# Output projection of a hybrid attention/GLA layer: five of seven products summed in shared PSUM banks, residual loads in slots of their own, the norm's root on ScalarE

## The chip, the cores and the metric

The program runs on one core of one Trainium2 chip. The metric is the device time of one execution in microseconds (us). Three runs of the kernel before gave 1463.15, 1465.78 and 1466.69 us; the median is 1465.78 us. One further execution was taken with the profiler; all rows below come from it.

## The reference, cut to what matters

The layer reads x (1024 tokens by 2048), projects it once, runs sliding-window attention and gated linear attention on the result, and ends with an output projection, a residual and a LayerNorm. Only the end is touched by this change:

```python
y = jnp.einsum('bse,ed->bsd', jnp.concatenate([y_a, y_g], axis=-1), w_out[l])   # 1024x2048 by 2048x2048
x = _layer_norm(DN_ALPHA * x + y, ln_g[l], ln_b[l])                             # per token, over 2048 columns

def _layer_norm(z, g, b):
    zf = z.astype(jnp.float32)
    mu = jnp.mean(zf, axis=-1, keepdims=True)
    var = jnp.mean(jnp.square(zf - mu), axis=-1, keepdims=True)
    return ((zf - mu) * lax.rsqrt(var + LN_EPS) * g + b).astype(z.dtype)
```

## The kernel before

**Numbers.** Everything is float32. An operand is split into a high part (a cast on ScalarE, L113) and a low part (a subtraction on VectorE, L114), and a product of two operands takes three matmuls: high by high (L740), high by the weight's low (L741), low by high (L742).

**Seven products.** The output projection starts at L690, after the projection, the attention and the GLA are done. It cuts tokens, inner width and columns into two halves each and replaces eight block products by seven, in the order 1, 6, 7, 4, 5, 3, 2. Each product works on one operand of y (512 tokens, 8 blocks k of the inner width; `y_part`, L709; sums of y blocks on GpSimd, L716) and one of the weights (`w_parts`, L719; four loads of 512 KB for each 512 columns). A product has two column halves, fp 0 and 1, and four token blocks t. Its loops are fp, k, t with three matmuls inside: 2 x 8 x 4 x 3 = 192 matmuls of 128x512. The very last half, product 2 with fp 1, runs token by token (t outside, k inside), so that a token block can be normed while the next is multiplied; three of its eight weights have slots of their own (`w2_p`, tiles vh and vl).

**Sums.** Each half of a product accumulates in four of eight PSUM banks (pool mm has 3, pool op has 5), and the next half uses the other four. `collect` (L774) adds each bank into the result tiles. `pre` has eight tiles of 128x2048, pre_11395 to pre_11398 for the first four token blocks and pre_11399 to pre_11402 for the last four. Columns 0 to 1023 of the first are called c11, the rest c12; of the second c21 and c22. x's columns 0 to 1023 are loaded into pre beforehand.

**Residual.** The second half of x's columns is added late (`residual`, L768): for the last four token blocks after product 5, for the first four after product 3. It loads 512 KB into a slot of `raw` (L771), adds it on VectorE (L772) and takes two statistics (L766). The pool `raw` has 4 slots, and all weight loads (L728 for products 1, 2, 3; L731 for the others) use the same four.

**Norm.** `norm` (L744) aggregates the statistics, gets the reciprocal root by a power on GpSimd (L454) with four small VectorE steps behind it (L455 to L458), and scales: 608 of the 2048 columns on ScalarE and GpSimd (L751, L752, L756, L757), 1440 on VectorE (L761, L762, in three pieces of 480 for the very last block). Stores follow each piece (L758, L763).

**What sets the order.** The engines run their instructions in the order of the program. A scheduler with its own timeline lays that order down, engine by engine; splits and loads have a high priority. All DMAs are issued by one engine (SP, its rows are SPq) in that order. An issue that waits for a free slot holds up all issues behind it.

Of the kernel before, what the change touches and what calls it, by code (L numbers as in the profile page):

```python
# [7 lines left out]
F32 = mybir.dt.float32  # L8
# [68 lines left out]
def build(ctx: ExitStack, tc, xT, xr, w_e, w_v, w_gk, w_up, b_gk, cos_d, sin_d, cst_d, sinks, wn_d, w_out, g_d, b_d, out):  # L77
# [615 lines left out]
    w2_p = ctx.enter_context(tc.tile_pool(name="w2", bufs=3, reuse_waits="tile"))  # L693
# [4 lines left out]
    mhalf2 = lp.tile([P, 1], F32, name="mhalf2")  # L698
    G.memset(mhalf2, -0.5)
    mh[0] = mhalf2  # L700
# [18 lines left out]
    def w_parts(i, fp, pools):  # L719

        out = []
        for q in range(4):
            r = raw_p.tile([P, 2, 512], F32, name="raw", tag="raw")
            with tc.high_priority(2000):
                if i in (1, 2, 3):
                    eg, w = {1: (fp, 0), 2: (fp, 2), 3: (2 + fp, 2)}[i]
                    src = w_out[eg, w + q // 2][:, (q % 2) * 1024:(q % 2) * 1024 + 1024]
                    SP.dma_start(r, src.rearrange("p (u c) -> p u c", u=2))  # L728
                else:
                    j = {5: 0, 7: 1, 4: 2, 6: 3}[i]  # L730
                    SP.dma_start(r.rearrange("p u (h c) -> p (u h) c", h=2), td[fp][:, 4 * q:4 * q + 4, j])  # L731
            for u in range(2):
                pool, tag = pools(2 * q + u)
                out.append(split(r[:, u], pool, tag))
        return out

    def product(acc, y, w, t, k):
        (yh, yl), (wh, wl) = y, w
        c = slice(t * P, t * P + P)
        PE.matmul(acc, yh[:, c], wh, start=(k == 0), stop=False)  # L740
        PE.matmul(acc, yh[:, c], wl, start=False, stop=False)  # L741
        PE.matmul(acc, yl[:, c], wh, start=False, stop=(k == 7))  # L742

    def norm(tb, tail):  # L744
        z, r0 = pre[tb], tb * P
        mv = lp.tile([P, 2], F32, name="mv", tag="mv", bufs=2)
        V.bn_aggr(mv, stats[tb])
        nmu = lp.tile([P, 1], F32, name="nmu", tag="nmu", bufs=2)
        V.tensor_scalar(nmu, mv[:, 0:1], -1.0, None, ALU.mult)
        p = slice(0, POOLED)  # L750
# [7 lines left out]
        SP.dma_start(out[r0:r0 + P, p], z[:, p])  # L758
        for a, m in cols:
            c = slice(a, a + m)  # L760
            V.scalar_tensor_tensor(z[:, c], z[:, c], mv[:, 0:1], gb[:, c], ALU.subtract, ALU.mult)  # L761
            V.scalar_tensor_tensor(z[:, c], z[:, c], rs, bb[:, c], ALU.mult, ALU.add)  # L762
            SP.dma_start(out[r0:r0 + P, c], z[:, c])  # L763
# [4 lines left out]
    def residual(tb):  # L768

        r = raw_p.tile([P, 1024], F32, name="raw", tag="raw")  # L770
        SP.dma_start(r, xr[tb * P:tb * P + P, 1024:])  # L771
        V.scalar_tensor_tensor(pre[tb][:, 1024:], r, ALPHA, pre[tb][:, 1024:], ALU.mult, ALU.add)  # L772
        for eg in (2, 3):
            stat(tb, eg)  # L774

    def collect(i, fp, t, acc):
        lo, hi = slice(fp * 512, fp * 512 + 512), slice(1024 + fp * 512, 1024 + fp * 512 + 512)
        c11, c12, c21, c22 = pre[t][:, lo], pre[t][:, hi], pre[NB + t][:, lo], pre[NB + t][:, hi]
        if i == 1:
            A.copy(c12, acc)  # L780
            V.scalar_tensor_tensor(c11, c11, ALPHA, acc, ALU.mult, ALU.add)
        elif i == 6:
            V.tensor_tensor(c12, c12, acc, ALU.add)
        elif i == 7:
            V.tensor_tensor(c22, c12, acc, ALU.add)
        elif i == 4:
            V.scalar_tensor_tensor(c21, c21, ALPHA, acc, ALU.mult, ALU.add)
            G.tensor_tensor(c21, c21, c22, ALU.add)
            stat(NB + t, fp)
        elif i == 5:  # L790
            V.tensor_tensor(c22, c22, acc, ALU.add)
            V.tensor_tensor(c12, c12, acc, ALU.add)
            if fp:
                residual(NB + t)
                norm(NB + t, False)
        elif i == 3:
            V.tensor_tensor(c12, c12, acc, ALU.add)
            if fp:
                residual(t)
        else:  # L800
            V.tensor_tensor(c11, c11, acc, ALU.add)
            stat(t, fp)
            if fp:
                norm(t, t == NB - 1)

    count = 0
    for n, i in enumerate((1, 6, 7, 4, 5, 3, 2)):
# [4 lines left out]
        if i == 7:  # L812
            SP.dma_start(gb, g_d)
            SP.dma_start(bb, b_d)
        ys = []
        for fp in range(2):
            accs = []
            for t in range(NB):
                pool, tag = (mm, "mm") if count % 8 < 3 else (op, "op")
                accs.append(pool.tile([P, 512], F32, name="acco", tag=tag))  # L820
                count += 1
            last = i == 2 and fp == 1
            ws = w_parts(i, fp, lambda k: (w2_p, "v") if last and k > 4 else (w_p, "w"))
            for k in range(8):
                if fp == 0:
                    ys.append(y_part(i, k))
                if not last:
                    for t in range(NB):
                        product(accs[t], ys[k], ws[k], t, k)
            for t in range(NB):  # L830
                if last:
                    for k in range(8):
                        product(accs[t], ys[k], ws[k], t, k)
                collect(i, fp, t, accs[t])
# [44 lines left out]
```

## Time and profile before

| what | value |
|---|---|
| runs of the kernel before | 1463.15, 1465.78, 1466.69 us |
| profiled execution, own time | 1466.27 us |
| its span, first to last instruction | 1464.4 us |
| PE busy in the span | 97% |
| VectorE, ScalarE, GpSimd busy | 61%, 41%, 25% |
| mean granted TensorE clock | 0.987 |

The span is what the engines show; 1466.27 - 1464.4 = 1.87 us of the execution lie outside of it. A clock of 1.00 means that TensorE was granted its full speed (the level of 2.4 GHz). Matmuls are pipelined: each takes 0.39 us from start to end, but one starts about every 0.23 us, so starts are what one counts by.

### The profile page before, as it was taken

To read this page: it belongs to the slowest core of one execution; us is meant where nothing else is said; L and a number is where in the kernel's file an instruction comes from. 1 tells how busy PE (TensorE), PEld (TensorE's weight loads), DVE (VectorE), ACT (ScalarE), POOL (GpSimd) and SP (SyncE) were. 2 spreads that over 40 slices of the span, in tenths; PEclk is the share of its full clock that TensorE was granted. 3 is DMA by queue.
4 is the path that set the end of the run, shared out by engine and by line. 5 is a ranking of instruction groups with operands and counts; after the bars stand their busy time and mean duration, and the time that the engine had idled before them with its cause. 6 is when DMAs were issued, how large, how long until landed. Compare 5 with 4: busy or idle time off the path is not lost.

```text
span 1464.4 us, 23613 instructions
## 1 busy us (share of the span) xinstructions
PE 1419.3 (97%) x8992; PEld 1183.5 (81%) x8992; DVE 886.2 (61%) x1522; ACT 605.9 (41%) x1278; POOL 370.4 (25%) x373
## 2 busy tenths in 40 slices
PE   8999999999999999999999999999999999997984
PEld 5888788888888977888889888888988888885763
DVE  5566556555655665566556555655565555567968
ACT  5544345434434554444335435443553434322321
POOL 0132211212221122232211221310023231465505
PEclk9999999999999999999999999999999999998987
DMA  8243344343434346443344343433235967666642
GB/s 311 94 150 113 126 131 145 120 132 127 148 109 137 117 158 214 138 138 123 122 145 137 123 132 119 148 108 115 94 113 179 360 204 222 192 217 210 215 130 115
DMA packets 101392, 224.47 MB, mean 153 GB/s; under 512 B 11040, under 2 KB 44192, under 8 KB 101024
## 3 DMA queue, kind: packets, MB, share of 16 engines
q1 hardware_dynamic: 101280, 222.98, 46.0%
q8 instruction: 70, 1.15, 0.3%
q14 instruction: 42, 0.34, 0.1%
HBM read 184.66 MB, written 33.55 MB: 149 GB/s over the span
## 4 chain that ended last, share of the span: by engine, by line
PE 92%; DVE 5%; DMA 1%; issue 1%; POOL 1%; ACT 0%; SPq 0%; DVEq 0%; ACTq 0%
PE acc L172 17%; PE acc L174 17%; PE acc L173 17%; PE acco L740 6%; PE acco L741 6%; PE acco L742 6%; PE accv L186 4%; PE accv L188 4%; PE accv L187 4%; PE po L291 2%; PE pa L360 1%; PE ps L260 1%; PE ps L259 1%; PE pt L281 1%; PE lracc L310 1%; DVE pre L762 1%
## 5 line engine op out<-in xcount | busy, mean ns | idle before, releaser
L114 DVE TENSOR_TENSOR wl<-raw,wh 128x512 fp32r<-128x512 f32 x445 | 344.4, 781 | 270.2 <-ACT wh L113 245.6
L113 ACT CAST wh<-raw 128x512 fp32r<-128x512 f32 x445 | 272.2, 620 | 444.5 <-PE acc L173 279.6
L172 PE MATMUL acc<-xh,wh 128*128 128x512 f32 x1088 | 429.4, 396 | 6.6 <-ACT wh L113 6.6
L174 PE MATMUL acc<-xh,wl 128*128 128x512 f32 x1088 | 426.6, 392 | 0.0
L173 PE MATMUL acc<-xl,wh 128*128 128x512 f32 x1088 | 426.5, 392 | 0.0
L172 PEld LDWEIGHTS acc<-xh,wh 128*128 128x128 f32 x1088 | 204.7, 188 | 53.8 <-ACT wh L113 7.6
L174 PEld LDWEIGHTS acc<-xh,wl 128*128 128x128 f32 x1088 | 204.6, 188 | 44.7 <-issue 1.4
L173 PEld LDWEIGHTS acc<-xl,wh 128*128 128x128 f32 x1088 | 204.8, 188 | 43.0 <-issue 2.2
L740 PE MATMUL acco<-wh,xh 128*128 128x512 f32 x436 | 168.0, 395 | 14.6 <-ACT wh L113 14.6
L741 PE MATMUL acco<-wl,xh 128*128 128x512 f32 x436 | 171.8, 394 | 3.9 <-DVE wl L114 3.9
L742 PE MATMUL acco<-wh,xl 128*128 128x512 f32 x436 | 171.0, 393 | 0.0
L186 PE MATMUL accv<-wh,xh 128*128 128x256 f32 x512 | 145.3, 284 | 0.0
L188 PE MATMUL accv<-wh,xl 128*128 128x256 f32 x512 | 145.0, 283 | 0.0
L187 PE MATMUL accv<-wl,xh 128*128 128x256 f32 x512 | 144.8, 283 | 0.0
L716 POOL TENSOR_TENSOR yr<-yr 128x512 f32<-128x512 f32 x56 | 79.6, 1424 | 150.1 <-DMA yr<-yd 145.3
L740 PEld LDWEIGHTS acco<-wh,xh 128*128 128x128 f32 x436 | 82.7, 190 | 32.7 <-ACT wh L113 15.5
L741 PEld LDWEIGHTS acco<-wl,xh 128*128 128x128 f32 x436 | 82.9, 190 | 22.0 <-DVE wl L114 4.6
L186 PEld LDWEIGHTS accv<-wh,xh 128*128 128x128 f32 x512 | 98.1, 192 | 1.2 <-issue 0.7
L188 PEld LDWEIGHTS accv<-wh,xl 128*128 128x128 f32 x512 | 98.1, 192 | 0.6 <-issue 0.3
L187 PEld LDWEIGHTS accv<-wl,xh 128*128 128x128 f32 x512 | 98.2, 192 | 0.5
L742 PEld LDWEIGHTS acco<-wh,xl 128*128 128x128 f32 x436 | 83.0, 190 | 17.3
L278 POOL TENSOR_TENSOR s<-s,sm 128x512 f32<-128x512 f32 x32 | 37.2, 1163 | 214.0 <-DVE sm L277 111.5
(173 smaller groups left out, 1707.2 us busy)
## 6 DMA issues: line engine op xcount, KB each, us to landing
raw<-in_w_e_dram SPq DMA_DIRECT2D x134, 512.0 KB, 3.9
yr<-yd SPq DMA_DIRECT2D x112, 256.0 KB, 4.8
raw<-in_w_v_dram SPq DMA_DIRECT2D x32, 512.0 KB, 4.4
raw<-in_w_out_dram SPq DMA_DIRECT2D x128, 128.0 KB, 2.6
td<-raw SPq DMA_DIRECT2D x32, 512.0 KB, 3.5
raw<-td SPq DMA_DIRECT2D x32, 512.0 KB, 4.3
raw<-in_w_out_dram SPq DMA_DIRECT2D x24, 512.0 KB, 4.5
raw<-in_xT_dram SPq DMA_DIRECT2D x15, 512.0 KB, 4.7
```

Of the source, the lines that this page charges most:

```text
L113: A.copy(hi, src)
L114: V.tensor_tensor(lo, src, hi.bitcast(F32), ALU.subtract)
L172: PE.matmul(acc, wh[:, c], xh, start=(k == 0), stop=False)
L173: PE.matmul(acc, wh[:, c], xl, start=False, stop=False)
L174: PE.matmul(acc, wl[:, c], xh, start=False, stop=(k == KT - 1))
L186: PE.matmul(o, xh[:, t], wh[:, c], start=(k == 0 and tb % 2 == 0), stop=False, skip_group_check=True)
L187: PE.matmul(o, xh[:, t], wl[:, c], start=False, stop=False, skip_group_check=True)
L188: PE.matmul(o, xl[:, t], wh[:, c], start=False, stop=(k == KT - 1), skip_group_check=True)
L716: G.tensor_tensor(a, a, b, ALU.add if sign > 0 else ALU.subtract)
L740: PE.matmul(acc, yh[:, c], wh, start=(k == 0), stop=False)
L741: PE.matmul(acc, yh[:, c], wl, start=False, stop=False)
L742: PE.matmul(acc, yl[:, c], wh, start=False, stop=(k == 7))
```

## The change

- Products 1, 6, 7, 4 accumulate in the same eight banks without a restart, then products 5 and 3 do; product 2 is alone. In between the running sum is copied out or added where it is complete: after product 1 into c11, after 6 to c12 (a ScalarE copy), after 7 to c22 (a ScalarE copy), after 4 into c21; after 5 into c22, after 3 into c12, after 2 into c11. The VectorE adds of products 6 (L783), 7 (L785) and one of product 5 (L792), the GpSimd add of product 4 (L788) and the ScalarE copy of product 1 (L780) are gone; the two new ScalarE copies are there.
- The residual is loaded into two slots of its own (pool `res`) and is added at products 7 and 4, no longer after 5 and 3. Statistics of the columns 1024 and up are taken as soon as products 5 and 3 are added.
- The root is ScalarE's Sqrt, followed by a reciprocal and three small steps on VectorE. ScalarE scales and shifts its 608 columns in one instruction instead of two; both GpSimd steps follow behind it.
- The last four token blocks are stored as whole tiles of 1 MB, issued behind the loads of product 2's first half. The first four are stored as before.
- The three extra weight slots of the last half are gone.

```diff
+    r_p = ctx.enter_context(tc.tile_pool(name="res", bufs=2, reuse_waits="tile"))
-    w2_p = ctx.enter_context(tc.tile_pool(name="w2", bufs=3, reuse_waits="tile"))
...
-    def product(acc, y, w, t, k):
+    def product(acc, y, w, t, k, first, last):
...
+        PE.matmul(acc, yh[:, c], wh, start=(first and k == 0), stop=False, skip_group_check=True)
+        PE.matmul(acc, yh[:, c], wl, start=False, stop=False, skip_group_check=True)
+        PE.matmul(acc, yl[:, c], wh, start=False, stop=(last and k == 7), skip_group_check=True)
...
-        nmu = lp.tile([P, 1], F32, name="nmu", tag="nmu", bufs=2)
-        V.tensor_scalar(nmu, mv[:, 0:1], -1.0, None, ALU.mult)
-        A.activation(z[:, p], z[:, p], AF.Identity, bias=nmu)
-        G.tensor_tensor(z[:, p], z[:, p], gb[:, p], ALU.mult)
-        rs = rsqrt(lp, mv[:, 1:2], 1.0, LN_EPS, 1)
-        A.activation(z[:, p], z[:, p], AF.Copy, scale=rs)
-        G.tensor_tensor(z[:, p], z[:, p], bb[:, p], ALU.add)
...
+        with tc.high_priority():
+            A.activation(q, mv[:, 1:2], AF.Sqrt, bias=eps)
+        V.tensor_scalar(v, mv[:, 1:2], -0.5, -0.5 * LN_EPS, ALU.mult, ALU.add)
+        V.scalar_tensor_tensor(z[:, c], z[:, c], mv[:, 0:1], gb[:, c], ALU.subtract, ALU.mult)
+        V.reciprocal(rs, q)
+        V.scalar_tensor_tensor(q, rs, v, rs, ALU.mult, ALU.mult)
+        V.scalar_tensor_tensor(rs, q, 1.5, rs, ALU.add, ALU.mult)
+        V.scalar_tensor_tensor(nmr, mv[:, 0:1], -1.0, rs, ALU.mult, ALU.mult)
+        A.activation(z[:, p], z[:, p], AF.Identity, bias=nmr, scale=rs)
...
+        G.tensor_tensor(z[:, p], z[:, p], gb[:, p], ALU.mult)
+        G.tensor_tensor(z[:, p], z[:, p], bb[:, p], ALU.add)
+        if tb < NB:
+            SP.dma_start(out[r0:r0 + P, p], z[:, p])
+        else:
+            late.append(lambda: tc.keep_in_program_order(SP.dma_start(out[r0:r0 + P, :], z)))
...
-        r = raw_p.tile([P, 1024], F32, name="raw", tag="raw")
+        r = r_p.tile([P, 1024], F32, name="res", tag="res")
...
+    FIRST, LAST = (1, 5, 2), (4, 3, 2)
...
         if i == 1:
-            A.copy(c12, acc)
             V.scalar_tensor_tensor(c11, c11, ALPHA, acc, ALU.mult, ALU.add)
         elif i == 6:
-            V.tensor_tensor(c12, c12, acc, ALU.add)
+            A.copy(c12, acc)
         elif i == 7:
-            V.tensor_tensor(c22, c12, acc, ALU.add)
+            A.copy(c22, acc)
         elif i == 4:
             V.scalar_tensor_tensor(c21, c21, ALPHA, acc, ALU.mult, ALU.add)
-            G.tensor_tensor(c21, c21, c22, ALU.add)
             stat(NB + t, fp)
         elif i == 5:
             V.tensor_tensor(c22, c22, acc, ALU.add)
-            V.tensor_tensor(c12, c12, acc, ALU.add)
+            stat(NB + t, 2 + fp)
             if fp:
-                residual(NB + t)
                 norm(NB + t, False)
         elif i == 3:
             V.tensor_tensor(c12, c12, acc, ALU.add)
-            if fp:
-                residual(t)
+            stat(t, 2 + fp)
...
+        if i in (7, 4):
+            for t in range(NB):
+                residual(t + (NB if i == 4 else 0))
...
+            if i == 2 and fp == 0:
+                for f in late:
+                    f()
```

The scheduler lays the order anew. On SP, before, from the last y loads of the projection on to the first store of the first four token blocks (raw<-in_xr_dram is a residual, raw<-in_w_out_dram at the end are the eight weight loads of product 2, two for one pair of k):

```order
L771 DMA raw<-in_xr_dram 128x1024
L706 DMA yr<-yd_3_115 128x512
L771 DMA raw<-in_xr_dram 128x1024 x2
L758 DMA out_dram<-pre_11399 128x608
L763 DMA out_dram<-pre_11399 128x1440
L706 DMA yr<-yd_3_115 128x512
L758 DMA out_dram<-pre_11400 128x608
L763 DMA out_dram<-pre_11400 128x1440
L771 DMA raw<-in_xr_dram 128x1024
L763 DMA out_dram<-pre_11401 128x1440
L758 DMA out_dram<-pre_11401 128x608
L763 DMA out_dram<-pre_11402 128x1440
```

In the changed kernel the same stretch of SP reads (L727 is the weight load, L705 the y load, L773 the store of a whole tile):

```order
L705 DMA yr<-yd_3_115 128x512
L727 DMA raw<-in_w_out_dram 128x1024
L705 DMA yr<-yd_3_115 128x512 x2
L727 DMA raw<-in_w_out_dram 128x1024
L705 DMA yr<-yd_3_115 128x512
L773 DMA out_dram<-pre_11399 128x2048
L773 DMA out_dram<-pre_11400 128x2048
L727 DMA raw<-in_w_out_dram 128x1024 x2
L773 DMA out_dram<-pre_11401 128x2048
L727 DMA raw<-in_w_out_dram 128x1024
L773 DMA out_dram<-pre_11402 128x2048
L727 DMA raw<-in_w_out_dram 128x1024
```

Before, all eight weight loads of product 2 stood behind the residual loads and the last store of pre_11402. Now the four of its first half stand ahead of the four stores (two of them are shown), and the four of its second half among and behind them.

The residual loads now stand in SP's row around product 7 (td are the stored weight sums that products 7 and 4 read; res is the new pool):

```order
L705 DMA yr<-yd_0_112 128x512
L705 DMA yr<-yd_0_116 128x512
L783 DMA res<-in_xr_dram 128x1024 x2
L705 DMA yr<-yd_1_113 128x512
L730 DMA raw<-td_111 128x4x256
L705 DMA yr<-yd_1_117 128x512
L783 DMA res<-in_xr_dram 128x1024 x2
L730 DMA raw<-td_110 128x4x256
L705 DMA yr<-yd_1_113 128x512
L705 DMA yr<-yd_1_117 128x512
```

The first two residual loads stand further up and find both slots empty; these two pairs and one more pair at product 4 wait until VectorE has added the residual whose slot they take.

On VectorE at the very end, between the third and the fourth token block, before (L801 adds the product, L766 and L747 are statistics, L761 and L762 the two scaling steps):

```order
L761 SCALAR_TENSOR_TENSOR pre_11397<-pre_11397,mv,gb 128x1440
L455 TENSOR_TENSOR rt<-rr 128x1
L801 TENSOR_TENSOR pre_11398<-pre_11398,acco 128x512
L456 TENSOR_TENSOR rt<-rt,rv 128x1
L766 BN_STATS stats_11406<-pre_11398 128x6
L457 TENSOR_SCALAR rt<-rt 128x1
L747 BN_AGGR mv<-stats_11406 128x2
L458 TENSOR_TENSOR rr<-rr,rt 128x1
L749 TENSOR_SCALAR nmu<-mv 128x1
L762 SCALAR_TENSOR_TENSOR pre_11397<-pre_11397,rr,bb 128x1440
L453 TENSOR_SCALAR rv<-mv 128x1
L761 SCALAR_TENSOR_TENSOR pre_11398<-pre_11398,mv,gb 128x480 x3
```

In the changed kernel (L810 adds the product, L778 and L745 are statistics, L754 and L765 the scaling steps, L756 to L759 what follows the root):

```order
L754 SCALAR_TENSOR_TENSOR pre_11397<-pre_11397,mv,gb 128x1440
L756 RECIPROCAL rr<-rt 128x1
L810 TENSOR_TENSOR pre_11398<-pre_11398,acco 128x512
L757 SCALAR_TENSOR_TENSOR rt<-rr,rv 128x1
L778 BN_STATS stats_11406<-pre_11398 128x6
L758 SCALAR_TENSOR_TENSOR rr<-rt,rr 128x1
L745 BN_AGGR mv<-stats_11406 128x2
L759 SCALAR_TENSOR_TENSOR nmr<-mv,rr 128x1
L765 SCALAR_TENSOR_TENSOR pre_11397<-pre_11397,rr,bb 128x1440
L752 TENSOR_SCALAR rv<-mv 128x1
L754 SCALAR_TENSOR_TENSOR pre_11398<-pre_11398,mv,gb 128x1440
```

The large steps stand as before. What changed is which small step stands between them, and that the fourth block's first scaling step is one of 1440 columns.

## Rows read from the trace of the kernel before

**Rows 1.** The chain that ended last, by engine, from the page.

```profile
PE 92%; DVE 5%; DMA 1%; issue 1%; POOL 1%; ACT 0%; SPq 0%; DVEq 0%; ACTq 0%
```

**Rows 2.** Windows from product 7 to the end; the columns stand in the first line.

```profile
core 0: us, PE busy (x) PEld busy (x) DVE busy (x) ACT busy (x) POOL busy (x), PEclk, DMA share, GB/s
1160.00:1332.50 172.50, 172.50 (x763) 142.82 (x761) 101.14 (x139) 54.25 (x95) 71.06 (x51) 1.00 0.68 217
...
1338.90:1349.40 10.50, 6.50 (x17) 4.69 (x18) 10.50 (x14) 4.79 (x10) 5.99 (x3) 0.56 0.82 266
1349.40:1389.20 39.80, 39.80 (x177) 32.79 (x175) 39.80 (x63) 14.77 (x24) 20.72 (x12) 1.00 0.63 213
1389.20:1403.10 13.90, 5.39 (x14) 4.10 (x14) 13.90 (x21) 3.42 (x6) 1.34 (x1) 0.63 0.89 273
```

**Rows 3.** PE's waits from 1120 us on: total us, times, longest.

```profile
PE acco L740 <- ACT wh L113: 14.6, 2, 8.5
PE acco L741 <- DVE wl L114: 3.9, 1, 3.9
```

**Rows 4.** Timeline of PE: start, duration, instruction.

```profile
1323.64 0.39 PE L742 MATMUL acco<-wh,xl 128*128 128x512 f32 x1
...
1332.48 0.39 PE L742 MATMUL acco<-wh,xl 128*128 128x512 f32 x1
...
1434.76 0.39 PE L741 MATMUL acco<-wl,xh 128*128 128x512 f32 x1
...
1444.00 0.40 PE L742 MATMUL acco<-vh,xl 128*128 128x512 f32 x1
```

**Rows 5.** SP's waits, 1300 to 1405 us.

```profile
SPq L728 <- DVE pre L772: 23.7, 8, 11.3
```

**Rows 6.** Groups of VectorE from 1060 us on: count, busy us, mean ns, idle before.

```profile
L772 DVE SCALAR_TENSOR_TENSOR pre<-raw,pre 128x1024 f32<-128x1024 f32 x8 | 10.8, 1354 | 0.0
...
L792 DVE TENSOR_TENSOR pre<-pre,acco 128x512 f32<-128x512 f32 x8 | 5.4, 679 | 0.0
```

**Rows 7.** The same groups of ScalarE: the copy out of PSUM.

```profile
L780 ACT COPY pre<-acco 128x512 f32<-128x512 f32 x8 | 4.3, 593 | 0.0
```

**Rows 8.** DMA issues: count, KB each, median us to landing.

```profile
yr<-yd SPq DMA_DIRECT2D x112, 256.0 KB, 4.8
...
raw<-in_xr_dram SPq DMA_DIRECT2D x8, 512.0 KB, 4.0
```

**Rows 9.** Timeline of GpSimd in product 7: the sum of two y blocks.

```profile
1215.82 1.51 POOL L716 TENSOR_TENSOR yr<-yr 128x512 f32<-128x512 f32 x1 [2.21 <-DMA yr<-yd]
```

**Rows 10.** ScalarE over the whole span: a table load.

```profile
L332 ACT ACT_TABLE_LOAD x8 | 10.3, 1283 | 0.2
```

**Rows 11.** Timeline of the end, VectorE, GpSimd and SP.

```profile
1447.01 1.46 POOL L752 TENSOR_TENSOR pre<-pre,gb 128x608 f32<-128x608 f32 x1
1447.07 1.41 DVE L455 TENSOR_TENSOR rt<-rr 128x1 f32<-128x1 f32 x1 [0.44 <-POOL rr L454]
1448.41 0.67 DVE L801 TENSOR_TENSOR pre<-pre,acco 128x512 f32<-128x512 f32 x1
...
1450.29 1.71 DVE L762 SCALAR_TENSOR_TENSOR pre<-pre,rr,bb 128x1440 f32<-128x1440 f32 x1
...
1451.10 2.21 POOL L757 TENSOR_TENSOR pre<-pre,bb 128x608 f32<-128x608 f32 x1 [2.63 <-ACT pre L756]
...
1451.97 4.32 DVE L761 SCALAR_TENSOR_TENSOR pre<-pre,mv,gb 128x480 f32<-128x480 f32 x3
...
1453.28 1.88 POOL L752 TENSOR_TENSOR pre<-pre,gb 128x608 f32<-128x608 f32 x1
...
1455.12 0.96 POOL L454 TENSOR_TENSOR rr<-rv,mhalf 128x1 f32<-128x1 f32 x1
1456.22 0.14 DVE L455 TENSOR_TENSOR rt<-rr 128x1 f32<-128x1 f32 x1
...
1460.68 0.38 SPq L758 DMA_DIRECT2D out_dram<-pre  x1
```

More of the change, by code (lines that the diff above doesn't have):

```diff
@@ L697, in build @@
     bb = lp.tile([P, D], F32, name="bb")
-    mhalf2 = lp.tile([P, 1], F32, name="mhalf2")
-    G.memset(mhalf2, -0.5)
-    mh[0] = mhalf2
+    eps = lp.tile([P, 1], F32, name="eps")
+    G.memset(eps, LN_EPS)
     def y_raw(h, g, k, tag):
@@ L732, in w_parts @@
             for u in range(2):
-                pool, tag = pools(2 * q + u)
-                out.append(split(r[:, u], pool, tag))
+                out.append(split(r[:, u], w_p, "w"))
         return out
-    def product(acc, y, w, t, k):
+    def product(acc, y, w, t, k, first, last):
         (yh, yl), (wh, wl) = y, w
         c = slice(t * P, t * P + P)
-        PE.matmul(acc, yh[:, c], wh, start=(k == 0), stop=False)
-        PE.matmul(acc, yh[:, c], wl, start=False, stop=False)
-        PE.matmul(acc, yl[:, c], wh, start=False, stop=(k == 7))
+        PE.matmul(acc, yh[:, c], wh, start=(first and k == 0), stop=False, skip_group_check=True)
+        PE.matmul(acc, yh[:, c], wl, start=False, stop=False, skip_group_check=True)
+        PE.matmul(acc, yl[:, c], wh, start=False, stop=(last and k == 7), skip_group_check=True)
     def norm(tb, tail):
@@ L804, in collect @@
                 norm(t, t == NB - 1)
+    accs = {}
     count = 0
-    for n, i in enumerate((1, 6, 7, 4, 5, 3, 2)):
+    for i in (1, 6, 7, 4, 5, 3, 2):
         if i in (1, 4):
@@ L814, in build @@
             SP.dma_start(bb, b_d)
+        if i in (7, 4):
+            for t in range(NB):
+                residual(t + (NB if i == 4 else 0))
         ys = []
         for fp in range(2):
[L817 to L823, printed above, removed]
+            if i in FIRST:
+                for t in range(NB):
+                    pool, tag = (mm, "mm") if count % 8 < 3 else (op, "op")
+                    accs[fp, t] = pool.tile([P, 512], F32, name="acco", tag=tag)
+                    count += 1
+            ws = w_parts(i, fp)
+            by_token = i == 2 and fp == 1
             for k in range(8):
@@ L826, in build @@
                     ys.append(y_part(i, k))
-                if not last:
+                if not by_token:
                     for t in range(NB):
-                        product(accs[t], ys[k], ws[k], t, k)
+                        product(accs[fp, t], ys[k], ws[k], t, k, i in FIRST, i in LAST)
+            if i == 2 and fp == 0:
+                for f in late:
+                    f()
             for t in range(NB):
-                if last:
+                if by_token:
                     for k in range(8):
-                        product(accs[t], ys[k], ws[k], t, k)
-                collect(i, fp, t, accs[t])
+                        product(accs[fp, t], ys[k], ws[k], t, k, True, True)
+                collect(i, fp, t, accs[fp, t])
 def layouts(x, w_in, w_gk_up, b_gk, attn_sinks, gla_norm_w, w_out, ln_g, ln_b):
```

16 lines of the change are left out of this document (9 added, 7 removed).

## The prediction, made before the changed kernel had run

> **What bounds the kernel now.** I read the chain that ended last first: TensorE holds 92% of it, VectorE 5% [rows 1]. So an edit counts only where it lets TensorE go on sooner, or shortens what follows its last matmul. Next come TensorE's waits in the output projection. There are three in all: 14.6 us in two waits for the high part of a weight (8.5 and 6.1), and 3.9 us in one for a low part [rows 3], together 18.5 us. The windows tell where. From 1160 to 1332.5, which holds nearly all of products 6, 7, 4 and 5, TensorE is busy without a gap at clock 1.00. The gaps lie at the two borders behind it: where product 3 starts (ends 1349.4) and where product 2 starts (ends 1403.1). In both windows VectorE has no idle time, and the granted clock is 0.56 and 0.63, so that TensorE runs part of them at its lower level, 1.2 GHz [rows 2].
>
> The waits of the queue SP say why the weights are late. At L728, the weight load, it waits 23.7 us in eight waits for L772, the residual's add on VectorE [rows 5]. The residual takes slots of the pool that the weights load into, is added only when VectorE gets to it, and until then the next weight load can't start.
>
> What the stalls cost in all can be counted. Between the starts at 1323.64 and 1332.48 lie 39 steps of TensorE [rows 4]: 0.2267 us each. In the by-token half, 40 steps from 1434.76 to 1444.00 give 0.231. Products 3 and 2 are 2 x 192 = 384 matmuls, 96 of them by token. Undisturbed they last 288 x 0.2267 + 96 x 0.231 = 65.3 + 22.2 = 87.5 us. They begin at 1332.48 + 0.23 = 1332.71 and the last ends at 1444.40, which is 111.7 us. So 24.2 us are lost: 18.5 as waits, and 5.7 by the lower clock behind them, 2.85 for each border.
>
> **The change, part by part.**
>
> *Residual out of the weights' slots.* At the border to product 3 VectorE loses, by mean durations, four adds of product 5's second half (L792, 4 x 0.679 = 2.7 us, gone) and four residual adds (L772, 4 x 1.354 = 5.4 us, now done beside product 4) [rows 6]; at the border to product 2 the other four residual adds, 5.4 us. The weight loads then depend only on the split that frees the slot, as they do in products 6 to 5, where TensorE never waits [rows 2, 3]. SP's order agrees: the weight loads stand among the y loads, and the first half of product 2 stands ahead of every store. I take both stalls as gone with their clock loss: **-24.2 us**. The bounds: nothing gained if the stalls came from the full VectorE alone (it is full in both windows), and no more than 24.2, since TensorE has no other gap here.
>
> *What is late next.* With the stalls gone TensorE does product 3 in 43.5 us (192 x 0.2267). I replayed the changed order by hand with the durations of the trace. VectorE has about 44 us of work beside product 3 (splits, four norms, adds, statistics), but splits go first by priority and the norms can slip: their stores stand behind the loads of product 2's first half, the norms end some 17 to 41 us after product 5, and the second half's weight loads behind the stores go out at 31 to 45 and are needed at 46 to 62. That is a slack of 10 us and more, so I cost the 1 MB stores at nothing. If that cover goes, the wait falls on the last half.
>
> *Residual loads at products 7 and 4.* Six of the eight are issued as three pairs that wait for VectorE's add of an earlier residual, and y loads for products 7 and 4 stand behind them. An add is 1.35 us [rows 6], the load 4.0 to land, a y load 4.8 [rows 8], the sum of two y blocks on GpSimd 1.5 [rows 9]. In the replay the operands k = 4 to 7 of product 7 are ready 2.6 to 3.7 us before TensorE needs them, because TensorE takes some of the second column half ahead of them. Product 6 has 1 to 2 us of slack at its last k. Cost nothing; bounds 0 and a wait at each of two places (rival C).
>
> *Shared banks.* Products 6 and 7 are copied out by ScalarE, 0.593 us a bank [rows 7], 2.4 for the four of a half, before the next product may add into them. Half a product is 96 x 0.2267 = 21.8 us, and ScalarE is under half busy in that stretch [rows 2]: nothing. The VectorE and GpSimd adds that go lie beside a TensorE that is never idle there: nothing gained.
>
> *The root on ScalarE.* The order has one more table load, ahead of the first Sqrt at the start of product 3, and none later. Table loads last 1.283 us with 0.2 us idle ahead of eight of them [rows 10]. ScalarE is idle for more than half of the windows around [rows 2], so I take nothing; the bounds are 0 and 1.5 us.
>
> The Trainium skill speaks against this step: "ScalarE: Activation LUTs", section "What ACT_TABLE_LOAD costs", counts a drain of about 1.4 us on top of the load for every switch to a function of another set, and exp and sqrt lie in different sets. By that the one switch would be an estimated 2.7 us of ScalarE instead of 1.5; nothing in the rows above shows the drain, and with one switch the sum stays the same.
>
> *The tail.* Before, the span ends 20.0 us after the last matmul (1444.40 to 1464.4); the fourth block's add of the product starts 4.0 us after it, the last store is issued at 16.3 [rows 11]. What fills the tail is VectorE and GpSimd holding each other off. A step of one column on VectorE (L455) took 1.41 us next to a GpSimd step of 608 columns, and 0.14 without one; three pieces of 480 took 4.32 while two GpSimd steps of 2.21 and 1.88 ran [rows 11]. One behind the other they fit: GpSimd ends at 1453.31, 1.3 us after VectorE's step of 1440 columns ended at 1452.00, and VectorE's pieces fill the rest. So I replay with 1.65 us for a VectorE step of 1440 columns, 1.3 for a GpSimd step of 608, one at a time, and 0.65 for an add or a statistic that overlaps with either. A token block then costs 2 x 1.65 + 2 x 1.3 = 5.9 us of such steps plus about 1.1 that nothing covers: 7.0. The power on GpSimd (0.96 alone [rows 11]) is gone, but reciprocal and three steps wait in the same way. Also, the first token block ends later: the low part of the last weight now comes late, and TensorE puts off that k, so block 0 ends at matmul 35 of 96, not 24. In the replay the fourth block's add starts 3.4 us after the last matmul, its statistics end at 5.8, its large step at 10.5, its last GpSimd step at 16 to 16.6. Before, the last store was issued at 16.3. **Tail: 0**, with bounds of -6 and +1.5 us; I take 0 because the rows with the overlap are of this very stretch.
>
> The Trainium skill has the rule behind it: "SBUF — State Buffer", section "Who interferes with whom", says that VectorE and GpSimd share a port pair which one holds for a whole instruction when a VectorE operation with two SBUF inputs meets GpSimd. The 1.41 us row agrees with it; without the rule the tail would be that of rival B.
>
> **Sum.** 1464.4 - 24.2 + 0 = 1440.2 us of span, plus 1.87 outside of it = 1442.1 for an execution like the profiled one. That one took 1466.27, 0.49 above the median of 1465.78; so the median of the changed kernel is about **1441.5 us**.
>
> **The rivals.**
>
> *B, the tail gets shorter too.* If VectorE and GpSimd don't hold each other as in the replay, the four blocks follow the multiplication (a block per 24 x 0.231 = 5.5 us). Then the last block has left about 0.5 to its add, 6 us of VectorE steps and 3.5 of ScalarE and GpSimd: about 10 instead of 16. For it: the power is gone, and both GpSimd steps come at the end. Against it: the 4.32 us row. 1441.5 - 6 = 1435.5.
>
> *C, a new wait in front of TensorE.* One residual pair that costs SP a whole landing and an add more than replayed is 4.0 + 1.35 = 5.4 us, against a slack of 2.6: a wait of 2.8, and 2.85 for the lower clock behind it as at the old borders. One such place gives 1447, both products 1453. For it: small slack, and an order that doesn't know the true durations. Against it: no wait there before [rows 2], when y loads were as many.
>
> *D, slower.* Each of the three pairs holds SP until VectorE has added, VectorE has splits of higher priority ahead of that add, and behind the pair stand the y loads of the product that runs. If each costs TensorE as much as the longest of the old waits, 8.5 us [rows 3], with 2.85 for the clock, it is 3 x 11.35 = 34 us against 24 saved: 1475.5. It decides only if all three do so (two give 1464, no change). Against it: VectorE is idle for 71 of the 172.5 us of that stretch [rows 2], so an add is not long in coming.
>
> *E, the stalls stay.* VectorE is full in both windows. If its queue and not the slots decides, its norms and statistics still stand there and TensorE waits on: about 1464. Against it: the 23.7 us that SP waits for the residual's add [rows 5], and 8.1 us less work at the first border.
>
> **How the numbers follow.** Forecast 0.60 (by itself 1438 to 1445), B 0.15, C 0.16, E 0.04, D 0.05. The range of 1434 to 1452 holds the first three but for a tenth. What a measurement of this kernel can tell from no change is about 0.3%, 4.4 us: the forecast, B and C are faster; E, with the part of D in which two pairs stall, is the same; the rest of D is slower. Faster 0.91, same 0.04, slower 0.05.
>
> **What would show it.** Right: no wait of TensorE of over 1 us between product 5 and the end, clock 1.00 throughout, the last matmul about 24 us earlier; no wait of SP at the weight load for a residual's add; the tail still near 20 us with VectorE steps of over 2 us beside GpSimd. Wrong: a wait of TensorE for a split of y in products 7 or 4 (C, D), a wait for a weight at products 3 or 2 with VectorE full (E), a tail under 17 us (B).

## The result, and the profile after

The changed kernel took 1455.97 us (median of 4 runs, 1455.35 to 1460.07) against 1464.65 for the kernel before on the same chip: a ratio of 0.9946 with a 95% interval of 0.9923 to 0.9969, some 8.7 us faster. The forecast was 1441.5 with a range of 1434 to 1452, so the direction was right, and only 8.7 of the 24 us forecast came. A second set of five runs gave 1457.13 (0.9937, 0.9925 to 0.9950). The profiled execution took 1460.07 us, its span is 1458.1; it is the longest of the first four runs, which matters below.

The chain that ended last, from the page, beside [rows 1]:

```profile
PE 90%; DVE 4%; DMA 3%; POOL 1%; issue 1%; ACT 1%; SPq 0%; POOLq 0%; DVEq 0%; ACTq 0%
```

Loads have come into the chain where there was 1% before. The waits of TensorE from 1120 us on (total, times, longest), beside [rows 3]:

```profile
PE acco L740 <- DVE xl L114: 7.9, 2, 4.9
PE acco L738 <- ACT xh L113: 4.4, 1, 4.4
```

Not one wait for a weight is left: all 18.5 us of [rows 3] are gone. In their place stand three waits, 12.3 us, for the other operand: the high and low parts of y. The windows of product 7, product 3, product 2 and the tail, in the columns of [rows 2], show where:

```profile
1202.60:1252.10 49.50, 45.09 (x193) 36.86 (x192) 23.51 (x32) 20.16 (x37) 7.42 (x6) 0.97 0.72 216
1339.30:1395.30 56.00, 48.11 (x194) 38.64 (x193) 50.86 (x76) 22.08 (x39) 24.38 (x15) 0.91 0.58 195
1395.30:1439.20 43.90, 43.90 (x194) 36.03 (x192) 35.58 (x55) 8.68 (x16) 10.61 (x6) 1.00 0.30 108
1439.20:1458.10 18.90, 0.00 (x0) 0.00 (x0) 14.12 (x18) 1.98 (x3) 11.79 (x6) 0.59 0.42 166
```

A product undisturbed takes 43.5 us. Product 7 took 6.1 more (4.4 of wait, the rest at a lower clock), product 3 took 12.4 more (7.9 of wait, the rest clock), product 2 none. The tail is 18.9. Against the forecast span of 1440.2 this adds up: 6.6 us later at the start of product 3 (6.1 from product 7 and 0.5 from before it), 12.4 in product 3, 1.1 less in the tail: 1458.1.

**Product 7.** Timelines of SP, GpSimd and ScalarE (start, duration, instruction; L783 is the residual load):

```profile
1207.72 1.47 SPq L783 DMA_DIRECT2D res<-in_xr_dram  x2
1209.28 0.38 SPq L705 DMA_DIRECT2D yr<-yd  x1
1209.76 0.38 SPq L730 DMA_DIRECT2D raw<-td  x1
1210.23 0.46 SPq L705 DMA_DIRECT2D yr<-yd  x1
...
1219.28 1.26 POOL L715 TENSOR_TENSOR yr<-yr 128x512 f32<-128x512 f32 x1 [12.67 <-DMA yr<-yd]
...
1220.58 0.62 ACT L113 CAST xh<-yr 128x512 fp32r<-128x512 f32 x1 [8.73 <-POOL yr L715]
```

The y load issued at 1210.23 lands at 1219.1, after 8.9 us, where the median of [rows 8] was 4.8. Ahead of it, within 2.5 us, went two residuals of 512 KB, a weight sum of 512 KB and another y load. TensorE waits for that block until 1221.25. The load was also issued late: it stands on SP behind the residual pair, and the pair waited 7.1 us for VectorE's add of an earlier residual, which frees the slot. SP's waits for that add from 1195 to 1225 us (total, times, longest):

```profile
SPq L783 <- DVE pre L784: 10.3, 4, 7.1
```

**Product 3.** Timelines of SP, GpSimd, ScalarE, VectorE and TensorE around its last two operands (k = 6 and 7):

```profile
1343.34 3.40 SPq L705 DMA_DIRECT2D yr<-yd  x4
...
1348.93 9.95 POOL L715 TENSOR_TENSOR yr<-yr 128x512 f32<-128x512 f32 x6 [3.35 <-DMA yr<-yd]
...
1353.35 0.62 ACT L113 CAST xh<-yr 128x512 fp32r<-128x512 f32 x1 [1.19 <-POOL yr L715]
...
1358.92 0.62 ACT L113 CAST xh<-yr 128x512 fp32r<-128x512 f32 x1 [3.72 <-POOL yr L715]
...
1353.45 2.64 DVE L754 SCALAR_TENSOR_TENSOR pre<-pre,mv,gb 128x1440 f32<-128x1440 f32 x1
...
1356.08 1.69 DVE L114 TENSOR_TENSOR wl<-raw,wh 128x512 fp32r<-128x512 f32 x1
1357.69 1.74 DVE L114 TENSOR_TENSOR xl<-yr,xh 128x512 fp32r<-128x512 f32 x1
...
1359.42 1.70 DVE L754 SCALAR_TENSOR_TENSOR pre<-pre,mv,gb 128x1440 f32<-128x1440 f32 x1
...
1362.83 1.71 DVE L765 SCALAR_TENSOR_TENSOR pre<-pre,rr,bb 128x1440 f32<-128x1440 f32 x1
1364.46 1.42 DVE L759 SCALAR_TENSOR_TENSOR nmr<-mv,rr 128x1 f32<-128x1 f32 x1
1365.81 1.71 DVE L765 SCALAR_TENSOR_TENSOR pre<-pre,rr,bb 128x1440 f32<-128x1440 f32 x1
1367.43 1.95 DVE L114 TENSOR_TENSOR xl<-yr,xh 128x512 fp32r<-128x512 f32 x1
...
1359.49 0.50 PE L740 MATMUL acco<-wh,xl 128*128 128x512 f32 x1 [3.00 <-DVE xl L114]
...
1369.44 1.22 PE L740 MATMUL acco<-wh,xl 128*128 128x512 f32 x2 [4.89 <-DVE xl L114]
```

The y loads of k = 7 go out 4 us after the product has started, the sums end at 1358.9, the high part at 1359.5. So its low part could have been there at 1360.2. In VectorE's row it stands behind both scaling steps of two norms, and ends at 1369.4. Besides, some of VectorE's steps are up to 1.1 us longer while GpSimd sums y (2.64 for 1.70, 1.69 and 1.74 for 0.68), and a sum takes 1.66 in place of the 1.29 of product 7.

How late was y itself? The high part of k = 6 ended at 1353.97, and a subtraction of 0.68 us right behind it would have ended at 1354.6. TensorE's last matmul before the wait started at 1356.10, so it got to that low part at 1356.3 and would not have waited. Ten starts of 0.227 us later, at 1358.6, it would have come to k = 7, whose high part was there at 1359.5. By this estimate y's own lateness is worth about 0.9 us of wait. The rest of the 7.9 comes from what stands ahead of the two splits in VectorE's row, the norms' steps above all. But y has no slack either.

**The tail** went as forecast, in the very manner: VectorE's large step next to GpSimd's, the three pieces, and the last store, beside [rows 11]:

```profile
1445.75 2.86 DVE L754 SCALAR_TENSOR_TENSOR pre<-pre,mv,gb 128x1440 f32<-128x1440 f32 x1
...
1450.25 3.18 DVE L765 SCALAR_TENSOR_TENSOR pre<-pre,rr,bb 128x480 f32<-128x480 f32 x3
...
1447.17 2.76 POOL L769 TENSOR_TENSOR pre<-pre,bb 128x608 f32<-128x608 f32 x1
...
1454.77 0.33 SPq L771 DMA_DIRECT2D out_dram<-pre  x1
```

### The profile page after: what moved, and what is told of

Its sections match the earlier page's. It is cut to its first block, busy times and chain, and to the rows that moved or that the text cites. A ratio compares the mean times of both kernels' runs of the same rounds, so it can differ in the third digit from the quotient of the medians.

```text
span 1458.1 us, 23538 instructions
## 1 busy us (share of the span) xinstructions
PE 1420.5 (97%) x8992; PEld 1185.0 (81%) x8992; DVE 870.9 (60%) x1488; ACT 607.9 (42%) x1287; POOL 346.1 (24%) x357
## 4 chain that ended last, share of the span: by engine, by line
PE 90%; DVE 4%; DMA 3%; POOL 1%; issue 1%; ACT 1%; SPq 0%; POOLq 0%; DVEq 0%; ACTq 0%
PE acc L172 18%; PE acc L174 17%; PE acc L173 17%; PE acco L740 5%; PE acco L738 4%; PE acco L739 4%; PE accv L186 4%; PE accv L188 4%; PE accv L187 4%; DMA yr<-yd 3%; PE po L291 2%; PE pa L360 1%; POOL yr L715 1%; PE ps L260 1%; PE ps L259 1%; DVE pre L754 1%
## 5 line engine op out<-in xcount | busy, mean ns | idle before, releaser
L740 PE MATMUL acco<-wh,xl 128*128 128x512 f32 x448 | 176.0, 395 | 7.9 <-DVE xl L114 7.9
L738 PE MATMUL acco<-wh,xh 128*128 128x512 f32 x448 | 175.4, 395 | 4.4 <-ACT xh L113 4.4
L739 PE MATMUL acco<-wl,xh 128*128 128x512 f32 x448 | 176.1, 393 | 0.0
L113 ACT CAST xh<-yr 128x512 fp32r<-128x512 f32 x56 | 34.7, 623 | 141.3 <-POOL yr L715 111.8
```

The source lines that it names most:

```text
L113: A.copy(hi, src)
L738: PE.matmul(acc, yh[:, c], wh, start=(first and k == 0), stop=False, skip_group_check=True)
L739: PE.matmul(acc, yh[:, c], wl, start=False, stop=False, skip_group_check=True)
L740: PE.matmul(acc, yl[:, c], wh, start=False, stop=(last and k == 7), skip_group_check=True)
```

## The experiments

Two theories for product 3: (1) the splits of y stand behind the norm's steps on VectorE; (2) y comes late, because its loads stand on SP behind weight loads that wait for a slot. For product 7, (3): the bunch of residual loads ahead of the y loads.

**again** is the changed kernel once more, without an edit.

> The changed kernel once more. Its profiled execution (1460.1 us) was 4.0 to 4.7 us longer than its three timed ones (1455.4 to 1456.1), and one of its three waits of TensorE, in product 7, is 4.4 us with a clock loss behind it. If that wait depends on how fast a y load lands, a second profile shows it shorter or not at all, and the timed runs stay near 1455.5. If it is there in every execution, the profile shows 4.4 us again. Both waits in product 3 (3.0 and 4.9 us) come from the order on VectorE and are there again.

Measured: 1457.13 (1454.5 to 1458.64). This profile is of a run of 1454.5 us; its waits of TensorE:

```profile
PE acco L740 <- DVE xl L114: 8.7, 2, 5.1
PE acco L738 <- ACT xh L113: 1.1, 2, 0.9
```

So product 3's waits are there in both profiles, and product 7's depends on the execution: 4.4 us in a run of 1460, 0.9 at most in a run of 1454.5. SP's waits for the residual's add, 1195 to 1225 us:

```profile
SPq L783 <- DVE pre L784: 6.5, 4, 3.3
```

The y load behind the pair landed after 8.3 us here and 8.9 before, nearly the same. What differs is how long SP stood in front of the pair: 3.3 us here, 7.1 before. From here on the kernel before is 1465.3 to 1466.2, and 1456 to 1457 is the changed kernel's time.

**no_norm**, the last four token blocks stored without their norm:

```diff
             if fp:
-                norm(NB + t, False)
+                late.append(lambda: tc.keep_in_program_order(
+                    SP.dma_start(out[(NB + t) * P:(NB + t) * P + P, :], pre[NB + t])))
```

> Leaves out the norm of the last four token blocks (they are stored as sums); everything else as in the changed kernel. Theory 1, the norms behind product 5 hold up the splits of product 3's last operands of y on VectorE: both waits in product 3 go with the clock loss behind them, 12.4 us in the profile, so about 1443.5. Theory 2, the y loads of product 3 come late on SP behind weight loads that wait for a slot, whatever VectorE does: the waits stay, about 1455.

Measured: 1451.60, ratio 0.9896 (0.9881 to 0.9911). Between the two. TensorE's waits:

```profile
PE acco L738 <- ACT xh L113: 7.5, 2, 3.8
```

One of the two (3.8) is product 7's. In product 3 one wait of 3.7 is left, now for the high part: with no norm there y itself is late. But its order on SP is another one: the last y loads go out at 1350.87, some 12 us into the product instead of 4, behind two weight loads. So both waits for the low part go with the norms, and the run does not show what the norms cost with the loads left where they were.

**norm_x37** holds the norms back:

```diff
-            if fp:
-                norm(NB + t, False)
...
                     ys.append(y_part(i, k))
+                    if i == 3 and k == 7:
+                        for t in range(NB):
+                            norm(NB + t, False, low[0])
...
-        V.bn_aggr(mv, stats[tb])
+        ins = V.bn_aggr(mv, stats[tb])
+        if after is not None:
+            order(ins, after)
```

(low[0] is the last low-part subtraction that was written.)

> The same work as the changed kernel; the four norms of the last token blocks may only start behind the split of product 3's last operand of y. Theory 1a, it was the place of the splits behind the norm's steps: no wait in product 3 and nothing in its place, about 1443.5. Theory 1b, VectorE has more to do than fits beside products 3 and 2 (50.9 us in 56.0 and 35.6 in 43.9, longer where GpSimd holds it off): the wait only moves, to the weights of product 3's second half, to product 2 or into the tail, 1449 to 1456.

Measured: 1450.30, 0.9898 (0.9882 to 0.9914), some 6 us better than the changed kernel. The time lies in the range of theory 1b, but not for its reason: the wait didn't move to weights or the tail, it became one for the high part of y. Of TensorE's waits the 6.3 is in product 3, the rest (2.8) in product 7. The waits, and SP's rows ahead of the last operand:

```profile
PE acco L740 <- ACT xh L115: 9.1, 3, 6.3
```

```profile
1341.34 9.88 SPq L729 DMA_DIRECT2D raw<-in_w_out_dram  x2
1351.31 1.80 SPq L707 DMA_DIRECT2D yr<-yd  x4
```

The order has changed as well: two weight loads now stand ahead of the last four y loads, and hold them up for 10 us; these go out 14 us into the product. With the norms out of its way the split ends 1.4 us after the sums (10.5 in the changed kernel), but now the loads are late, as theory 2 has it.

**res3**: three residual slots.

```diff
-    r_p = ctx.enter_context(tc.tile_pool(name="res", bufs=2, reuse_waits="tile"))
+    r_p = ctx.enter_context(tc.tile_pool(name="res", bufs=3, reuse_waits="tile"))
```

> Three residual slots in place of two. Theory 3, the wait in product 7 comes from the residual loads that SP issues in a bunch ahead of the y loads: with a third slot one load goes out earlier and the bunch is smaller, the wait is shorter or gone, and the time falls by up to 5.7 us where the wait was there, to 1450. Rival: the timed runs never had it; 1455.5, no change.

Measured: 1443.38 (1441.89 to 1443.62), 0.9845 (0.9832 to 0.9858): twice the gain expected at best. TensorE's only wait:

```profile
PE acco L738 <- ACT xh L113: 0.5, 1, 0.5
```

It cures product 7, as expected, and product 3 too, which it should not touch. The order that came with it shows why: the last operand's split stands ahead of both second scaling steps, though its sums end at 1350.2, 16.7 us after the start of product 3 (19.6 in the changed kernel). VectorE:

```profile
1352.39 0.68 DVE L114 TENSOR_TENSOR xl<-yr,xh 128x512 fp32r<-128x512 f32 x1
...
1355.13 1.71 DVE L765 SCALAR_TENSOR_TENSOR pre<-pre,rr,bb 128x1440 f32<-128x1440 f32 x1
...
1358.75 1.71 DVE L765 SCALAR_TENSOR_TENSOR pre<-pre,rr,bb 128x1440 f32<-128x1440 f32 x1
```

It ends 19.6 us after the start; the product gets to that operand at 19 to 20. It is just in time, with nothing to spare.

**wres2**: weights of products 5, 3, 2 through the idle residual slots.

```diff
+            if i in (5, 3, 2) and q in (1, 3):
+                r = r_p.tile([P, 1024], F32, name="res", tag="res").rearrange("p (u c) -> p u c", u=2)
+            else:
+                r = raw_p.tile([P, 2, 512], F32, name="raw", tag="raw")
```

> The changed kernel, but the second and fourth weight load of each half of products 5, 3 and 2 go into the two residual slots, which are idle after product 4: six slots for weights instead of four. In the changed kernel SP waited 26.4 us in six waits at weight loads between 1296 and 1346 us, with y loads of product 3 behind them. Theory 2, the y loads are late because they stand behind weight loads that wait for a slot: the waits of TensorE in product 3 go, those in product 7 stay as they were (0.9 to 4.4 us), about 1444. Theory 1, the splits of y stand behind the norm's steps on VectorE, whatever SP does: about 1455, no change.

Measured: 1458.15, 0.9933 (0.9910 to 0.9956): no change from the changed kernel. But SP was not freed, so it doesn't speak against theory 2. SP's waits from 1290 to 1365 us at these weight loads (31.6 in the changed kernel):

```profile
SPq L730 <- DVE wl L114: 33.8, 9, 8.9
```

Two more slots did not shorten the wait for the splits that free them. In this kernel the last operand's sums end at 1360.1 and its split at 1369.9, with two norms in between: theory 1.

**wres3**, the same with three slots:

> Three residual slots, and weight loads of products 5, 3, 2 in two of four cases through them. With three slots alone TensorE had one wait of 0.5 us left and the time was 1443.4. Nothing is left to gain ahead of the last matmul but that 0.5: 1442.5 to 1443.5 if the order holds; if the gain of the third slot was a matter of one lucky order, a wait of some us comes back somewhere, 1446 to 1455.

Measured: 1454.93, 0.9919 (0.9901 to 0.9938). Product 7 is cured (0.8), product 3 waits 7.5 again. So the second expectation holds: the gain of res3 in product 3 hung on its order.

**wres3n**, with the norms held back as in norm_x37:

> As wres3, and the four norms behind product 5 may only start behind the split of product 3's last operand of y. If the norm's place only mattered because y was late, nothing changes: 1442.5 to 1443.5. If VectorE then runs out of time beside product 2, the last norms slip into the end and the tail grows beyond 19 us: 1445 to 1450.

Measured: 1448.39, 0.9871 (0.9847 to 0.9895), 6.5 better than wres3; the tail did not grow. In product 3 one wait of 5.1 for the high part is left, as in norm_x37, and the last y loads again go out some 14 us into the product. Holding the norms back helps, and it lays the loads later; no run holds the norms back and leaves the loads where they were.

**b_res**, one part of the change put into the kernel before (the three weight slots of the last half go too):

```diff
-    w2_p = ctx.enter_context(tc.tile_pool(name="w2", bufs=3, reuse_waits="tile"))
+    r_p = ctx.enter_context(tc.tile_pool(name="res", bufs=2, reuse_waits="tile"))
...
-        r = raw_p.tile([P, 1024], F32, name="raw", tag="raw")
+        r = r_p.tile([P, 1024], F32, name="res", tag="res")
```

> The kernel before with one part of the change: residuals in two slots of their own, still after products 5 and 3, with separate sums, the old norm and no extra weight slots for the last half. The reason of the prediction (residuals in the weights' slots make the weights late) says that both old stalls go even so: 24 us less than before, about 1442 to 1446. The rival, VectorE has too much to do at the two borders (it had no idle time there), says that the stalls stay for the most part: 1455 to 1466.

Measured: 1459.50, 0.9952 (0.9939 to 0.9964). The time is the rival's. TensorE's waits, and the windows of products 3 and 2 and the tail:

```profile
PE acco L742 <- DVE xl L114: 4.1, 2, 2.6
PE acco L740 <- ACT xh L113: 3.0, 1, 3.0
PE acco L741 <- DVE wl L114: 1.5, 2, 0.8
```

```profile
1333.60:1388.10 54.50, 47.38 (x194) 37.95 (x192) 49.45 (x67) 18.00 (x30) 36.09 (x22) 0.94 0.63 206
1388.10:1435.10 47.00, 45.20 (x194) 35.65 (x192) 46.55 (x75) 11.70 (x19) 11.70 (x7) 1.00 0.39 141
1435.10:1458.90 23.80, 0.00 (x0) 0.00 (x0) 18.73 (x30) 3.90 (x5) 12.49 (x7) 0.60 0.44 176
```

The waits are not the rival's: of the 18.5 us for weights in [rows 3] 1.5 are left, in product 2. In their place product 3 loses 11 us to y, product 2 loses 3, and the tail is 3.8 us longer than before. VectorE is full (46.55 of 47.00) in product 2. Slots of their own take the old waits away, and alone they bring new ones.

**wact2**: product 3's weights are loaded from ScalarE's queue.

```diff
-                    SP.dma_start(r, src.rearrange("p (u c) -> p u c", u=2))
+                    (A if i in (3,) else SP).dma_start(r, src.rearrange("p (u c) -> p u c", u=2))
```

> The changed kernel, but the eight weight loads of product 3 are issued by ScalarE's queue instead of SP's, so that no y load of product 3 stands behind a weight load that waits for a slot. Six slots instead of four (wres2) had not helped, since SP still waited 33.8 us at weight loads. Theory 2 (y late on SP): the operands of product 3 are summed well before they are needed, the waits in product 3 go and only those of product 7 stay, 1443 to 1448. Theory 1 (splits behind the norm's steps on VectorE): the last split of y still ends some 28 us after product 3 starts and TensorE waits again, 1454 to 1458.

Measured: 1450.68, 0.9895 (0.9880 to 0.9909). TensorE's waits, the first in product 3, the second in product 7, and VectorE's rows up to the last split:

```profile
PE acco L740 <- DVE xl L114: 3.0, 1, 3.0
PE acco L738 <- ACT xh L113: 1.9, 1, 1.9
```

```profile
1352.14 1.71 DVE L765 SCALAR_TENSOR_TENSOR pre<-pre,rr,bb 128x1440 f32<-128x1440 f32 x1
1353.77 1.45 DVE L759 SCALAR_TENSOR_TENSOR nmr<-mv,rr 128x1 f32<-128x1 f32 x1
1355.15 1.71 DVE L765 SCALAR_TENSOR_TENSOR pre<-pre,rr,bb 128x1440 f32<-128x1440 f32 x1
...
1358.85 1.78 DVE L114 TENSOR_TENSOR xl<-yr,xh 128x512 fp32r<-128x512 f32 x1
```

The sums now end at 1350.0, 13.5 us after the start of product 3 in place of 19.6: y is early. Its split still ends 10.7 us later, behind the norms: ScalarE's cast starts at 1353.07, behind a step of a norm, and VectorE's subtraction follows the rows above. So earlier loads took 7.9 us of waits in product 3 to 3.0, and the norms make the rest.

**wact3**, the same with three slots:

> wact2 with three residual slots. If theory 2 holds and the third slot takes the wait out of product 7, no wait is left: 1441 to 1443.5, as with three slots alone, but now with time to spare in product 3. If three slots alone were a lucky order, this shows a wait in product 3 again: 1446 to 1455.

Measured: 1441.86 (1441.39 to 1443.51), 0.9839 (0.9825 to 0.9854). Waits of 1.1 and 0.8 are left.

**wact3n**, with the norms held back as well:

> wact3 with the four norms behind product 5 held back until the split of product 3's last operand of y. With y early that split comes early and the norms start at about the same time: 1441 to 1443.5. If the norm's steps still come into the way of weight splits: a wait for a weight's low part, 1445 to 1450.

Measured: 1443.07, 0.9846 (0.9830 to 0.9863). TensorE's wait from 1120 us on, and the window of product 3:

```profile
PE acco L740 <- ACT xh L115: 0.2, 1, 0.2
```

```profile
1333.40:1377.00 43.60, 43.60 (x194) 36.09 (x194) 41.16 (x65) 18.51 (x33) 17.25 (x10) 1.00 0.64 214
```

The sums end 12.2 us after the start of product 3 and the split at 13.9, where TensorE gets to it at 19 to 20. With product 2 at 43.9 us and a tail of 18.9 the span is 1439.8, near the 1440.2 of the prediction. In time wact3, res3 and wact3n can't be told apart.

**tail_nopool**, for the tail:

```diff
-        G.tensor_tensor(z[:, p], z[:, p], gb[:, p], ALU.mult)
-        G.tensor_tensor(z[:, p], z[:, p], bb[:, p], ALU.add)
+        if tb not in (0, 1, 2):
+            G.tensor_tensor(z[:, p], z[:, p], gb[:, p], ALU.mult)
+            G.tensor_tensor(z[:, p], z[:, p], bb[:, p], ALU.add)
```

> The changed kernel without GpSimd's two steps on the first three token blocks (their first 608 columns lack gain and offset); the last stored block keeps them. In the changed kernel the span ends 18.9 us after TensorE's last matmul and VectorE's steps of 1440 columns take 2.86 us beside GpSimd. If the two hold each other off, the steps of the blocks in between fall to about 1.7 us, VectorE keeps up with the matmuls, and the tail is 13.5 to 15.5 us. If the end is set by the last block's own chain whatever the blocks before it do, the tail stays 18 to 19.

Measured: 1452.17 in its one run. TensorE's last matmul ends at 1436.7, the span at 1450.3: a tail of 13.6, from 18.9. VectorE's large steps for the last two blocks:

```profile
1434.72 1.71 DVE L754 SCALAR_TENSOR_TENSOR pre<-pre,mv,gb 128x1440 f32<-128x1440 f32 x1
...
1440.03 1.71 DVE L754 SCALAR_TENSOR_TENSOR pre<-pre,mv,gb 128x1440 f32<-128x1440 f32 x1
```

1.71 in place of 2.86, with GpSimd out of the way. The two do hold each other off, and that is worth 5.3 us of tail, near the 6 that rival B had for a tail without it.

## Why the prediction was wrong

*Old stalls (-24.2): right in the part they play.* All waits for weights are gone. b_res bears the reason out: with the residuals in slots of their own 1.5 of the 18.5 us are left. But it gains 6.7 us, not 24, because new waits for y and a longer tail come in. Which other part of the change keeps product 2 and the tail free of them was not tested part by part; that it is the VectorE work that the shared sums drop is argued from VectorE's busy time in product 2 alone (46.55 of 47.00 us in b_res, 35.58 of 43.90 in the changed kernel).

*"What is late next": the step that failed.* It said that VectorE's 44 us beside product 3 don't matter, since "splits go first by priority and the norms can slip". The priority acts when the order is laid down, by times that the scheduler assumes. On the chip the row is fixed: a split stands where it stands. In VectorE's row of the changed kernel the split of product 3's last operand is behind two whole norms. I had replayed that order, but with steps of their lone durations, GpSimd's sums at 1.5 us, and y at 4.8 us, and found no wait. The rows say 1.66 for a sum, up to 1.1 us more for a VectorE step next to one, and y loads that go out 4 us into the product. Cost: 12.4 us in product 3 in the first profile and 12.2 in the second. That it is the norms' place is shown by the rows of the changed kernel (a split 10.5 us behind its sums, and y itself late by an estimated 0.9) and by norm_x37 against again and wres3n against wres3 (some 6 us each in time; 3.3 and 4.4 us in product 3 of their profiles, where the loads moved too). That y had no slack to bear it is shown by wact2 (waits of 7.9 down to 3.0 with the weights off SP). With both, and the third slot, 0.2 is left (wact3n).

A detail of it: I used that VectorE and GpSimd hold each other off for the tail, with rows, and it was right there (18.9 against 20.0 forecast, shown by tail_nopool). Product 3 has 24 sums of y on GpSimd, of which nine run beside it, and 24 splits and four norms on VectorE; there I did not use it.

*Residual loads at product 7 (0): mis-sized.* This is rival C's place and its mechanism, priced at a wait of 2.8 us and 2.85 of clock. Measured with two slots: a longest wait of 0.9 to 4.6 from run to run, with 1.7 of clock behind one of 4.4. Two terms were too small. A y load was put at 4.8 us; behind the residuals it landed after 7.3 to 8.9 in all seven profiles with two slots. And VectorE's add was put at 1.35 us; SP stood up to 7.9 us for it. TensorE's longest wait in product 7 goes with SP's longest wait for the add:

| run | SP for the add, us | TensorE, us |
|---|---|---|
| again | 3.3 | 0.9 |
| wact2 | 4.6 | 1.9 |
| norm_x37 | 5.0 | 1.9 |
| no_norm | 6.0 | 3.8 |
| first profile | 7.1 | 4.4 |
| tail_nopool | 7.7 | 4.3 |
| wres2 | 7.9 | 4.6 |
| three slots, five runs | 2.8 to 3.3 | 0.2 to 0.8 |

With three slots the y load lands as late, after 6.3 to 8.7 us, but SP gets to it sooner. That VectorE is idle for much of this stretch, which the prediction held against D, did not bring the add early: in the first profile VectorE idled 5.2 us in front of the split of an earlier operand (1204.16), and the add stands behind that split in its row (1205.38). Product 4's pair cost nothing in any run.

*The rest:* the shared banks, the copies, the table load, the 1 MB stores and the by-token half cost nothing visible, as said. The table load took 1.28 us.

The Trainium skill, "ScalarE: Activation LUTs", section "What ACT_TABLE_LOAD costs", puts a drain of about 1.4 us on top for every switch to another set. No run here shows it: in res3 ScalarE's cast ended at 1343.12, the load ran from 1343.14 to 1344.42, and the Sqrt started at 1344.43, so that the switch cost 1.3 us.

The Trainium skill, "SBUF — State Buffer", section "Who interferes with whom", says that a VectorE instruction with two SBUF inputs contends with a GpSimd instruction that reads SBUF. The tail agrees: 2.86 us beside GpSimd, 1.71 without.

*Rivals.* B and E did not happen, but E's reason, that VectorE's queue decides, came true for the y of product 3 in place of weights. D did not happen either: the longest wait behind a residual pair was 4.6 (wres2). C got one place right, and its range for one place and a second one (1447 to 1453) was too low, as the second place, product 3, was not in it. In the chances, a part of D is counted under "the same" in words, but all of its 0.05 stands under "slower".

*Still open:* what the norms' place costs with the loads unmoved was estimated and not run; and why three slots alone bring product 3's split forward in the order is known only as a fact of that order; it was not traced inside the scheduler.

## What to carry to other kernels

When a stall goes, walk the operand that comes next through every queue it passes (its load on the DMA queue, its sum, its casts), in the new order and with durations taken where the same engines ran together, and ask what stands ahead of it in each row. A scheduler's priority says nothing about a row that is already laid down. A load that waits for its slot holds up the small loads behind it on the same queue, and large loads issued just ahead of a small one make it land later: price both. An idle engine does not free a slot early when the step that frees it stands behind another that waits. And a single execution can hide or show such a wait, so look at two.

## What the hardware showed that was not expected

The same kernel's wait in product 7 was 4.4 us in one execution and 0.9 in another, with the same order: SP stood 7.1 us at a residual load in one and 3.3 in the other, while the y load behind it landed after 8.9 and 8.3. In the kernel before the median of the y loads was 4.8 ([rows 8]). A one-column VectorE step (L759) took 1.42 us beside GpSimd and 0.15 without. In the changed kernel's first profile TensorE ran at the lower clock in part of the stretch behind the waits in product 3 (starts 0.43 us apart in place of 0.23; granted 0.91 over the window), and 7.9 us of waits cost 12.4. In wact2 a wait of 3.0 in product 3 cost 3.3 (granted 1.00).
